# Product pairs in turns by k tile, norm steps two products apart, and bias loads ahead of the first queries

## The chip, the cores and the metric

The kernel runs on one core of a Trainium2 chip. The metric is the device time of one execution in microseconds, from which the median of several runs is taken. All stretches below are microseconds from the start of the profiled span.

## What is computed

Two transformer-like blocks run one after the other on 512 tokens of width 1024, in float32. The first block is a normed input product into three mixers (a gated convolution of width 31 with a norm per head, a short gated convolution, a spatial gating with a norm per head), an output product, a layer of 16384 experts chosen by product keys, and a gated projection. The second block is a state-space mixer with a gated output product, a convolutional feed-forward layer, a gated projection, a differential attention with relative bias, a second feed-forward layer and a second gated projection. Cut to what the change touches:

```python
def group_layernorm(x, g, b, heads):                  # the mixers' norm per head
    m = jnp.mean(xf, axis=-1, keepdims=True)
    var = jnp.mean(jnp.square(xf - m), axis=-1, keepdims=True)
    ...
z = rmsnorm(h, g_mix[i]) @ w_in[i]                    # and so each stage: norm, then products
y = causal_dwconv(val * jax.nn.sigmoid(gate), w)      # 31 taps, then group_layernorm, then silu
mixed = jnp.einsum("hij,bnjhc->bnihc", ws, vb) + b_s  # after group_layernorm of v
bias = rel_bias[t5_causal_bucket(rel)]                # tables used by the attention, much later
```

## The kernel before

Activations lie with features on partitions: eight k tiles of 128 features by 512 tokens. A weight strip holds 128 output features for all eight k tiles. Each float32 product is made of three matmuls of reduced form (L161 high weights by high input, L162 low weights by high input, L163 high weights by low input). The high half of a weight strip is copied by ScalarE (L148, `wh`), the low half is the difference made by VectorE or, for strips marked `pool`, by GpSimd (L150, `wl`). The input's high half is made by ScalarE (L117, L119), its low half by VectorE (L112, L114). So L163 is the matmul that waits when an input tile comes late.

The order on every engine is the order in which the program issues; nothing reorders it. Time in the program is counted in ticks, one after each product of eight k tiles (24 matmuls). `later(n, f)` runs `f` n ticks on, `lin` makes one product, and `done` ticks, puts the product's follow-up one tick on and runs some background work from `self.bg`. `lin2` makes the first two products of a stage and leaves their last k tile to the end, because the tile of the previous stage that is finished last is k tile 7. It is called ten times: mixers (L527, with `first=True`), expert queries, the three gated projections, the state-space input, the gated output product, the two feed-forward layers, the attention queries. Only with `first=True` do the two products go in turns, the second two k tiles behind the first; otherwise the first product's k tiles 0 to 6 go ahead of the second's. Behind the first product's last tile stands the norm's sum over features (L240), behind the second's its spread over partitions (L252); the follow-ups need both.

`head_ln` (L332) is the mixers' norm of one head pair: mean by a matmul (L339, `pmn`), centring on VectorE and squaring on ScalarE one tick on, `two_rms` one tick on (L361 `psv`, a root, a reciprocal and a split on VectorE into `rl`), then the turn (L374, `pst`) one tick on and the spread (L381, `psb`) one tick on. It runs for three tiles of the convolution (issued one tick after the last of 31 taps, L442, `cacc`) and three of the gating (`vv`). Seven taps are issued per product as background work. `two_rms` is also used by the attention's norms, with a lag of one tick.

In the expert stage the background list begins with `bias_prep` (L1740): GpSimd loads `rel_bias`, negates it, then loads the buckets and the lambdas; eight tables (`head`, L1761 on TensorE) and one small step follow; writes of zeros (L655) are set between them, and a copy of an index table comes last.

Of the kernel before, what the change touches and what calls it, by code (L numbers as in the profile page):

```python
# [14 lines left out]
ALU = mybir.AluOpType  # L15
# [21 lines left out]
class K:  # L37
# [142 lines left out]
            c = slice(k * P, k * P + P)  # L180
            self.mm3(ps, s.hi[:, c], s.lo[:, c], *rhs[k], k == 0, k == len(rhs) - 1)

    def lin2(self, rhs, *posts, first=False):

        n = len(rhs)
        ss = [self.next_strip(), self.next_strip(self.LA - 1)]
        pss = [self.mm() for _ in posts]
        if first:
            for k in range(n + 1):
                for i, j in ((0, k), (1, k - 2)):  # L190
                    if 0 <= j < n - 1:
                        self.prod(pss[i], ss[i], rhs, j, j + 1)
        else:
            for s, ps in zip(ss, pss):
                self.prod(ps, s, rhs, 0, n - 1)
        for s, ps, post in zip(ss, pss, posts):
            self.prod(ps, s, rhs, n - 1, n)
            self.done(post, ps)
# [133 lines left out]
    def head_ln(self, y, out):  # L332

        nc = self.nc
        d = {}

        def mean():
            d["m"] = self.px_(name="pmn")
            nc.tensor.matmul(d["m"], self.bd64, y, start=True, stop=True)  # L339
            self.later(1, center)  # L340

        def center():
            nc.vector.tensor_tensor(y, y, d["m"], ALU.subtract)
            d["sq"] = self.tmp(tag="sq")
            nc.scalar.activation(d["sq"], y, AF.Square)
            self.later(1, lambda: self.two_rms(d["sq"], self.sel2, 1.0, scale))

        def scale(psb):
            yn = self.tmp(tag="yn")
            nc.vector.tensor_tensor(yn, y, psb, ALU.mult)  # L350
            out(yn)

        mean()

    def two_rms(self, sq, sel, scale, out):

        nc = self.nc
        d = {}
        ps = self.px_((P, NB, 2), "psv")
        for b in range(NB):  # L360
            nc.tensor.matmul(ps[:, b, :], sq[:, b * P : b * P + P], sel, start=True, stop=True)  # L361
        r = self.sp.tile([P, NB, 2], F32, tag="rl", name=self.name("rl"), bufs=3)
        nc.scalar.activation(r, ps, AF.Sqrt, scale=scale, bias=self.eps)
        r2 = self.sp.tile([P, NB, 2], F32, tag="rl2", name=self.name("rl2"), bufs=3)
        nc.vector.reciprocal(r2, r)

        r4 = self.sp.tile([P, NB, 4], F32R, tag="rl4", name=self.name("rl4"), bufs=3)
        nc.vector.tensor_copy(r4[:, :, 0:2], r2)
        nc.vector.tensor_tensor(r4[:, :, 2:4], r2, r4.bitcast(F32)[:, :, 0:2], ALU.subtract)

        def turn():
            pst = self.px_((4, NB, P), "pst")
            for b in range(NB):
                nc.tensor.transpose(pst[:, b, :], r4.bitcast(F32)[:, b, :], self.ident)  # L374
            d["t"] = self.tmp((4, T), F32R, tag="rT")
            nc.scalar.copy(d["t"], pst.rearrange("p a b -> p (a b)"))
            self.later(1, spread)

        def spread():
            psb = self.px_(name="psb")  # L380
            nc.tensor.matmul(psb, self.selT, d["t"], start=True, stop=True)  # L381
            out(psb)

        self.later(1, turn)

    TAPS = 7
    W_IN_ORDER = [0, 3, 1, 15, 4, 2, 16, 8, 5, 17, 10, 6, 12, 9, 11, 13, 7, 14]
# [11 lines left out]
    def mix_in(self, after):  # L399
        nc, I = self.nc, self.I  # L400
# [10 lines left out]
        xn = self.rhs(self.xn[0])  # L411
# [20 lines left out]
        def conv(j, sg):  # L432
            y = self.loc(tag="ypad", bufs=3)
            nc.vector.tensor_tensor(y, st["val", j], sg, ALU.mult)
            acc = self.loc(tag="cacc", bufs=3)

            def tap(k):
                w, o = cw[:, j * 31 + k : j * 31 + k + 1], 30 - k
                if k == 30:
                    nc.scalar.activation(acc, y, AF.Identity, scale=w, bias=cb[:, j : j + 1])  # L440
                else:
                    nc.vector.scalar_tensor_tensor(out=acc[:, o:], in0=y[:, : T - o], scalar=w, in1=acc[:, o:], op0=ALU.mult, op1=ALU.add)  # L442
                if k == 0:
                    self.later(1, lambda: self.head_ln(acc, lambda yn: ln_a(j, yn)))

            tap(30)
            self.bg += [(1, lambda k=k: tap(k)) for k in range(29, -1, -1)]

        def ln_a(j, yn):
            nc.scalar.activation(yn, yn, AF.Silu, scale=self.v("ln_a_g")[:, j : j + 1], bias=self.v("ln_a_b")[:, j : j + 1])  # L450
            self.split(mix[:, j, 0, :], mix[:, j, 1, :], yn)
# [67 lines left out]
        posts = {}  # L519
# [4 lines left out]
        self.bg_rate, self.credit = self.TAPS, 0  # L524
        self.norm_stat(st)
        o = self.W_IN_ORDER
        self.lin2(xn, posts[o[0]], posts[o[1]], first=True)  # L527
        for m in o[2:]:
            self.lin(xn, posts[m])
        self.run_bg(1000)  # L530
# [93 lines left out]
    def peer(self):  # L624
        nc, I = self.nc, self.I
# [12 lines left out]
        iota = self.loc((P, P), tag="iota")  # L638
        nc.scalar.dma_start(iota, I["c_iota"])

        iotaP = self.bank("mmc", (P, P), "held")
# [3 lines left out]
        sq = self.tc.tile_pool(name="pq", bufs=1)  # L645
        self.st = sq.__enter__()
        sk = self.loc((P, 16, P), tag="sk")
        nc.scalar.dma_start(sk, I["skT"])
        self.bg = self.bias_prep() + [(0.1, lambda: nc.scalar.copy(iotaP, iota))]
        zero = self.loc((P, 112), tag="zero")  # L650
        nc.gpsimd.memset(zero, 0.0)
        zd = self.m1d.rearrange("g c t m -> (g c t) m").rearrange("(p b) m -> p b m", p=P)[:, :, 0:112]
        for i in range(8):
            o = zd[:, 8 * i : 8 * i + 8, :]
            self.bg.insert(2 * i + 1, (0, lambda o=o: nc.gpsimd.dma_start(o, zero.unsqueeze(1).to_broadcast([P, 8, 112]))))  # L655
        n = self.ap.tile([P, KT, 2, TD], F32R, tag="xn", name="n", bufs=2)
# [1084 lines left out]
    def bias_prep(self):  # L1741

        nc, I = self.nc, self.I
        self.bd = self.dp.tile([8, P, 640], F32, name="biasd")
        rb = self.loc((33, 8), tag="rb")
        oh = self.loc((33, 640), tag="rboh")
        lq = self.loc((P, 4, 64), tag="lq")
        self.nlam = self.cp.tile([P, 1], F32, name="nlam")

        def loads():  # L1750
            nc.gpsimd.memset(rb, 1e30)
            nc.gpsimd.dma_start(rb[0:32, :], I["rel_bias"])
            nc.gpsimd.tensor_scalar(out=rb[0:32, :], in0=rb[0:32, :], scalar1=-1.0, scalar2=None, op0=ALU.mult)
            nc.gpsimd.dma_start(oh, I["c_buckets"])
            nc.gpsimd.dma_start(lq, I["lam"])

        def head(h):
            o = self.loc((P, 640), tag="rbo", bufs=2)
            for a, b in ((0, 512), (512, 640)):
                ps = self.px_(name="pb")  # L1760
                nc.tensor.matmul(ps[:, 0 : b - a], rb[:, h : h + 1].to_broadcast([33, P]), oh[:, a:b], start=True, stop=True)  # L1761
                nc.scalar.copy(o[:, a:b], ps[:, 0 : b - a])
            nc.gpsimd.dma_start(self.bd[h], o)

        def lam():
            pr = self.loc((P, 2, 64), tag="lpr")
            nc.vector.tensor_tensor(pr, lq[:, 0:2], lq[:, 2:4], ALU.mult)
            sm = self.loc((P, 2), tag="lsm")
            nc.vector.tensor_reduce(sm, pr, AX.X, ALU.add)
            nc.scalar.activation(sm, sm, AF.Exp)  # L1770
            nc.vector.tensor_tensor(self.nlam, sm[:, 1:2], sm[:, 0:1], ALU.subtract)
            nc.vector.tensor_scalar(out=self.nlam, in0=self.nlam, scalar1=-self.LAM_INIT, scalar2=None, op0=ALU.add)

        return [(0.1, loads)] + [(0.1, lambda h=h: head(h)) for h in range(8)] + [(0.1, lam)]

    def head_rms(self, y, gain, then):

# [403 lines left out]
```

## Time and profile before

| what | value |
|---|---|
| median of 3 runs | 3077.76 us (3073.26 to 3085.12) |
| profiled execution | 3078.27 us, span 3076.5 us |
| mean granted TensorE clock | 0.971 of full speed |
| TensorE busy | 95% of the span |
| VectorE, ScalarE, GpSimd busy | 72%, 42%, 36% |

The page gives shares over the whole span. The stages have different limits, so the change is read stage by stage: from the list of who waits for whom, then from sums over stretches, then from the instructions in order of time. In a timeline a row is start, duration, engine, line, operation, what it writes and reads, how many are merged, and in brackets the idle time ahead of it and what ended it. A matmul's duration overlaps with the next; what one costs is the distance between starts, 0.227 us at the full clock of 2.4 GHz and 0.427 us at 1.2 GHz.

### The profile page before, as it was taken

The page shows a single profiled execution, that of the slowest core. Times are in us where ns is not written, and L with a number is a line of the kernel's source. Part 1 is how long each engine was busy: PE and PEld are TensorE (multiplying, and loading weights), DVE is VectorE, ACT ScalarE, POOL GpSimd, SP SyncE. Part 2 cuts the span into 40 slices and gives each one's busy share as a digit, 9 for nine tenths or more (in the row PEclk, how much of TensorE's full clock was granted, in tenths as well). Part 3 has the DMA queues.
Part 4 walks back from the last instruction along what each step waited for, and adds up shares of the span by engine and source line. Part 5 has one row for each costly group of instructions (what it writes and reads, how often), then busy time and mean ns, then how long its engine had stood idle before and what let it go on. Part 6 is the DMA issues. An engine that isn't in the chain of part 4 may idle for free. (4 is left out here: it accounts for less than half of the span.)

```text
span 3076.5 us, 39413 instructions
## 1 busy us (share of the span) xinstructions
PE 2908.9 (95%) x14359; PEld 2445.6 (79%) x14359; DVE 2218.9 (72%) x3788; ACT 1303.4 (42%) x2209; POOL 1093.8 (36%) x936
## 2 busy tenths in 40 slices
PE   8999988889999999999999979999999998999998
PEld 6677888788887888888787768888877766888886
DVE  7945888986888889988886674666666356566665
ACT  4333246566433433443335343433344345433333
POOL 3224566653248778877872321000011011100001
PEclk9889999899999999999999989999999989999999
DMA  4124335679778988898894473233332211333323
GB/s 140 48 83 148 97 129 186 232 245 313 252 263 313 336 318 322 331 350 315 312 328 147 125 225 103 77 102 99 99 97 95 77 42 42 96 103 96 96 72 99
DMA packets 235067, 534.77 MB, mean 174 GB/s; under 512 B 35135, under 2 KB 127683, under 8 KB 222202
## 3 DMA queue, kind: packets, MB, share of 16 engines
q1 hardware_dynamic: 170570, 343.69, 33.9%
q0 software_dynamic: 24832, 140.74, 12.4%
q10 hardware_dynamic: 39472, 47.84, 4.5%
q8 instruction: 113, 1.85, 0.2%
q14 instruction: 80, 0.66, 0.1%
HBM read 468.75 MB, written 63.44 MB: 173 GB/s over the span
## 5 line engine op out<-in xcount | busy, mean ns | idle before, releaser
L150 DVE TENSOR_TENSOR wl<-wr,wh 128x1024 fp32r<-128x1024 f32 (+2 forms) x453 | 545.3, 1213 | 510.1 <-ACT wh L148 509.9
L148 ACT ACTIVATE wh<-wr 128x1024 fp32r<-128x1024 f32 (+2 forms) x552 | 544.7, 995 | 403.7 <-PE mm L163 196.2
L161 PE MATMUL mm<-xn,wh 128*128 128x512 f32 x1296 | 520.9, 402 | 14.3 <-ACT xn L119 8.9
L163 PE MATMUL mm<-xn,wh 128*128 128x512 f32 x1296 | 512.4, 395 | 5.8 <-DVE xn L114 5.8
L162 PE MATMUL mm<-xn,wl 128*128 128x512 f32 x1296 | 512.1, 395 | 1.9 <-POOL wl L150 1.9
L230 POOL TENSOR_TENSOR accs<-accs,sq 128x512 f32<-128x512 f32 x56 | 86.3, 1541 | 1042.7 <-ACT sq L229 1038.4
L1112 PE MATMUL pv<-wh,A 128*128 128x512 f32 x1536 | 437.5, 397 | 15.8 <-ACT A L117 5.9
L150 POOL TENSOR_TENSOR wl<-wr,wh 128x1024 fp32r<-128x1024 f32 x99 | 241.3, 2439 | 449.1 <-ACT wh L148 446.6
L161 PE MATMUL mm<-n,wh 128*128 128x384 f32 x1024 | 350.6, 342 | 0.8 <-ACT gs L705 0.8
L162 PE MATMUL mm<-n,wl 128*128 128x384 f32 x1024 | 345.6, 337 | 5.9 <-DVE wl L150 4.3
L1112 PEld LDWEIGHTS pv<-wh,A 128*128 128x128 f32 x1536 | 286.8, 189 | 80.6 <-DVE A L112 11.0
L163 PE MATMUL mm<-n,wh 128*128 128x384 f32 x1024 | 345.9, 338 | 3.1 <-DVE n L114 3.1
L161 PEld LDWEIGHTS mm<-xn,wh 128*128 128x128 f32 x1296 | 248.5, 192 | 69.3 <-ACT xn L119 8.9
L163 PEld LDWEIGHTS mm<-xn,wh 128*128 128x128 f32 x1296 | 247.7, 191 | 61.4 <-DVE xn L114 8.3
L162 PEld LDWEIGHTS mm<-xn,wl 128*128 128x128 f32 x1296 | 248.4, 192 | 55.2 <-POOL wl L150 2.3
L1112 PE MATMUL pv<-wl,A 128*128 128x512 f32 x768 | 241.9, 396 | 9.4 <-DVE wl L150 9.3
L117 ACT ACTIVATE A<-ga 128x384 fp32r<-128x384 f32 x128 | 67.3, 526 | 357.7 <-DVE ga L1076 357.7
L162 PEld LDWEIGHTS mm<-n,wl 128*128 128x128 f32 x1024 | 194.2, 190 | 9.7 <-DVE wl L150 5.6
L161 PEld LDWEIGHTS mm<-n,wh 128*128 128x128 f32 x1024 | 194.5, 190 | 4.9 <-issue 1.4
L163 PEld LDWEIGHTS mm<-n,wh 128*128 128x128 f32 x1024 | 194.0, 189 | 3.4 <-DVE n L114 3.4
L1112 PEld LDWEIGHTS pv<-wl,A 128*128 128x128 f32 x768 | 144.0, 189 | 49.0 <-DVE wl L150 17.3
L1670 ACT ACTIVATE uc<-up,vec 128x512 f32<-128x512 f32 x88 | 71.8, 816 | 203.8 <-DVE up L1668 203.8
(414 smaller groups left out, 5438.9 us busy)
## 6 DMA issues: line engine op xcount, KB each, us to landing
wr<-in_exp_u SPq DMA_DIRECT2D x128, 512.0 KB, 5.4
wr<-in_exp_v SPq DMA_DIRECT2D x128, 512.0 KB, 6.9
wr<-in_w_up SPq DMA_DIRECT2D x88, 512.0 KB, 3.6
gd<-gb ACTq DMA_DIRECT2D x48, 512.0 KB, 5.0
G<-gd SPq DMA_DIRECT2D x32, 768.0 KB, 6.3
wr<-in_w_dn SPq DMA_DIRECT2D x64, 320.0 KB, 2.9
wr<-in_w_pg SPq DMA_DIRECT2D x24, 512.0 KB, 4.2
sd<-gs SPq DMA_DIRECT2D x56, 192.0 KB, 2.9
```

The lines of the kernel that those rows point to most:

```text
L117: nc.scalar.activation(hi, src, AF.Copy)
L148: nc.scalar.activation(s.hi, s.raw, AF.Copy)
L150: eng.tensor_tensor(s.lo, s.raw, s.hi.bitcast(F32), ALU.subtract)
L161: t.matmul(ps, wh, xh, start=start, stop=False)
L162: t.matmul(ps, wl, xh, start=False, stop=False)
L163: t.matmul(ps, wh, xl, start=False, stop=stop)
L230: self.later(1, lambda: nc.gpsimd.tensor_tensor(acc, acc, sq, ALU.add))
L1112: nc.tensor.matmul(pv[2 * b + h], a[:, x, o], w[:, h * T : h * T + T], start=(e == 0 and i == 0 and w is s.hi), stop=last)
L1670: nc.scalar.activation(c, u, AF.Identity, scale=w(2), bias=cb[:, m : m + 1])
```

## The change

`lin2` always goes in turns, and the switch `first` is gone. In the mixers' norm the turn is issued two ticks after `two_rms` instead of one, and a convolution's norm two ticks after its last tap instead of one. The three bias loads are issued at the start of the expert stage, ahead of the first query product, with `rel_bias` last; the negation is a background step of its own and on VectorE; the copy of the index table is the first background step.

```diff
-    def lin2(self, rhs, *posts, first=False):
+    def lin2(self, rhs, *posts):
...
-        if first:
-            for k in range(n + 1):
-                for i, j in ((0, k), (1, k - 2)):
-                    if 0 <= j < n - 1:
-                        self.prod(pss[i], ss[i], rhs, j, j + 1)
-        else:
-            for s, ps in zip(ss, pss):
-                self.prod(ps, s, rhs, 0, n - 1)
+        for k in range(n + 1):
+            for i, j in ((0, k), (1, k - 2)):
+                if 0 <= j < n - 1:
+                    self.prod(pss[i], ss[i], rhs, j, j + 1)
...
-            self.later(1, lambda: self.two_rms(d["sq"], self.sel2, 1.0, scale))
+            self.later(1, lambda: self.two_rms(d["sq"], self.sel2, 1.0, scale, 2))
...
-    def two_rms(self, sq, sel, scale, out):
+    def two_rms(self, sq, sel, scale, out, lag=1):
...
-        self.later(1, turn)
+        self.later(lag, turn)
...
-                    self.later(1, lambda: self.head_ln(acc, lambda yn: ln_a(j, yn)))
+                    self.later(2, lambda: self.head_ln(acc, lambda yn: ln_a(j, yn)))
...
-        self.bg = self.bias_prep() + [(0.1, lambda: nc.scalar.copy(iotaP, iota))]
+        bias, loads = self.bias_prep()
+        loads()
+
+        self.bg = [(0.1, lambda: nc.scalar.copy(iotaP, iota))] + bias
...
         def loads():
+            nc.gpsimd.dma_start(oh, I["c_buckets"])
+            nc.gpsimd.dma_start(lq, I["lam"])
             nc.gpsimd.memset(rb, 1e30)
             nc.gpsimd.dma_start(rb[0:32, :], I["rel_bias"])
-            nc.gpsimd.tensor_scalar(out=rb[0:32, :], in0=rb[0:32, :], scalar1=-1.0, scalar2=None, op0=ALU.mult)
-            nc.gpsimd.dma_start(oh, I["c_buckets"])
-            nc.gpsimd.dma_start(lq, I["lam"])
+
+        def negate():
+            nc.vector.tensor_scalar(out=rb[0:32, :], in0=rb[0:32, :], scalar1=-1.0, scalar2=None, op0=ALU.mult)
...
-        return [(0.1, loads)] + [(0.1, lambda h=h: head(h)) for h in range(8)] + [(0.1, lam)]
+        return [(0.1, negate)] + [(0.1, lambda h=h: head(h)) for h in range(8)] + [(0.1, lam)], loads
```

## Rows read from the trace of the kernel before

**Rows 1.** The page: busy time, share of the span and instructions of each engine.
```profile
PE 2908.9 (95%) x14359; PEld 2445.6 (79%) x14359; DVE 2218.9 (72%) x3788; ACT 1303.4 (42%) x2209; POOL 1093.8 (36%) x936
```
**Rows 2.** TensorE's waits over the span: total, times, longest, in microseconds.
```profile
PE pmn L339 <- DVE cacc L442: 6.2, 1, 6.2
...
PE mm L163 <- DVE xn L114: 5.8, 5, 2.4
```
**Rows 3.** Sums over stretches, pair to L240: length, busy (instructions), clock, DMA, GB/s.
```profile
225.04:235.24 10.20, 10.20 (x47) 8.45 (x45) 3.50 (x3) 3.48 (x4) 7.86 (x8) 1.00 0.61 201
1667.26:1678.23 10.97, 10.52 (x47) 8.37 (x45) 9.04 (x8) 6.57 (x10) 7.65 (x5) 1.00 0.09 19
1720.71:1737.40 16.69, 13.68 (x46) 10.43 (x45) 11.24 (x11) 9.88 (x15) 11.69 (x9) 0.80 0.02 10
...
2343.22:2356.33 13.11, 10.79 (x47) 8.34 (x45) 10.03 (x12) 7.01 (x10) 4.33 (x3) 1.00 0.17 52
```
**Rows 4.** Timeline, state-space pair: TensorE's wait, VectorE's low halves, GpSimd's last sum.
```profile
1728.71 0.79 PE L163 MATMUL mm<-xn,wh 128*128 128x512 f32 x1 [2.41 <-DVE xn L114]
...
1726.90 3.44 DVE L114 SCALAR_TENSOR_TENSOR xn<-x,gfs,xn 128x512 fp32r<-128x512 f32 x2
...
1731.44 2.25 POOL L1982 TENSOR_TENSOR accs<-accs,sq 128x512 f32<-128x512 f32 x1
```
**Rows 5.** Timeline, attention's pair: TensorE's wait, its norm steps, VectorE's low halves.
```profile
2350.52 0.50 PE L163 MATMUL mm<-xn,wh 128*128 128x512 f32 x1 [2.03 <-DVE xn L114]
...
2358.76 0.48 PE L161 MATMUL mm<-xn,wh 128*128 128x512 f32 x1
...
2348.72 3.45 DVE L114 SCALAR_TENSOR_TENSOR xn<-x,vec,xn 128x512 fp32r<-128x512 f32 x2
```
**Rows 6.** Timeline of VectorE: the second strip's low half in the second gated projection.
```profile
2289.78 1.72 DVE L150 TENSOR_TENSOR wl<-wr,wh 128x1024 fp32r<-128x1024 f32 x1
```
**Rows 7.** Timeline of the expert stage's start: GpSimd's bias loads, TensorE.
```profile
232.71 0.73 POOL L1752 DMA_DIRECT2D rb<-in_rel_bias  x1 [0.31 <-POOL rb L1751]
236.78 0.24 POOL L1753 TENSOR_SCALAR rb<-rb 32x8 f32<-32x8 f32 x1 [3.34 <-DMA rb<-in_rel_bias]
...
235.24 0.95 PE L240 MATMUL px<-ones,accs 128*128 128x1 f32 x8
239.52 2.13 PE L1761 MATMUL pb<-rboh,rb 33*128 33x512 f32 x4 [3.34 <-DMA rboh<-in_c_buckets]
...
254.18 1.05 PE L679 MATMUL sc<-sk,q 128*128 128x128 f32 x8
...
255.16 2.42 PE L1761 MATMUL pb<-rboh,rb 33*128 33x512 f32 x8
```
**Rows 8.** Sums over two stretches behind that wait, columns as in rows 3.
```profile
236.20:250.12 13.92, 10.60 (x26) 7.15 (x27) 1.47 (x3) 5.24 (x11) 5.70 (x8) 0.63 0.43 129
250.12:260.00 9.88, 9.88 (x46) 7.50 (x45) 4.42 (x24) 3.24 (x8) 6.82 (x7) 1.00 0.58 199
```
**Rows 9.** Sums over stretches of the mixers, columns as in rows 3 (TensorE, weights, VectorE, ...).
```profile
37.60:154.40 116.80, 106.18 (x464) 79.18 (x462) 112.83 (x138) 37.64 (x50) 33.61 (x14) 0.91 0.19 61
...
72.63:79.46 6.83, 5.16 (x11) 2.64 (x12) 6.62 (x11) 1.53 (x2) 2.51 (x1) 0.50 0.15 59
...
113.40:185.40 72.00, 72.00 (x291) 48.91 (x291) 51.40 (x72) 25.31 (x34) 7.61 (x3) 0.79 0.16 52
```
**Rows 10.** Timeline, mixers: TensorE's first wait; VectorE around it; a split by GpSimd.
```profile
74.30 1.01 PE L374 MATMUL pst<-ident,rl 128*4 128x128 f32 x4 [3.76 <-DVE rl L369]
...
74.06 0.68 DVE L417 TENSOR_TENSOR vv<-mm,rstd 128x512 f32<-128x512 f32 x1
74.67 7.25 DVE L442 SCALAR_TENSOR_TENSOR cacc<-ypad,vec,cacc 128x483 f32<-128x483 f32 x7
...
82.43 5.41 DVE L442 SCALAR_TENSOR_TENSOR cacc<-ypad,vec,cacc 128x506 f32<-128x506 f32 x7
...
76.95 2.84 POOL L150 TENSOR_TENSOR wl<-wr,wh 128x1024 fp32r<-128x1024 f32 x1 [6.13 <-ACT wh L148]
```

More of the change, by code (lines that the diff above doesn't have):

```diff
@@ L526, in mix_in @@
         o = self.W_IN_ORDER
-        self.lin2(xn, posts[o[0]], posts[o[1]], first=True)
+        self.lin2(xn, posts[o[0]], posts[o[1]])
         for m in o[2:]:
```

## Prediction

> **What bounds the kernel now.** I read the shares of the page first: TensorE is busy for 95% of the span [rows 1], so its holes are all that a change of order can give back. Then the list of TensorE's waits, in which the change aims at three kinds: the low half of an input tile that comes late at a stage's start (5.8 us, five times), the convolution's last tap (6.2 us, once) [rows 2], and the start of the expert stage, where TensorE waits 3.34 us for a DMA [rows 7]. Then sums over stretches, to see what each wait costs behind it: after the DMA wait the granted clock is 0.63 in the mean over 13.92 us, though nothing is idle there but the 3.34 us, and 1.00 in the stretch after it [rows 8]. So a wait costs its own time and half of the time for which the clock then stands at 1.2 instead of 2.4 GHz. Last the timeline of each place. The mixers differ from the rest: from 37.60 to 154.40 VectorE is busy for 112.83 of 116.80 us [rows 9], so there VectorE is the limit and TensorE's waits are its shadow.
>
> **The pairs in turns.** Nine pairs change; the mixers' pair already goes so. The work, the strips and their DMAs are the same and are issued at the same point, so no queue but TensorE's changes. Unhindered, the 45 matmuls up to L240 take 10.20 us [rows 3], 0.227 us each. In turns, k tile 6 of the first product comes eleventh instead of seventh, and its L163 starts 32 matmuls in, after 7.25 us, instead of 20 in, after 4.5 us; 13 matmuls (2.95 us) follow it to L240.
> The second strip is needed 2.0 us in instead of 4.8. The nearest case is the second gated projection: its low half ends at 2291.50 [rows 6], the pair starts 2290.60, so it is needed at 2292.6. No new wait.
> In six of the nine pairs nothing is late (the first line of rows 3 stands for them): nought.
> First gated projection: 10.97 against 10.20 us [rows 3]; 0.7 us gained, 0 to 0.8.
> Attention: tile 6 would be asked for at 2343.22 + 7.25 = 2350.47 and is there at 2350.52; L240 comes at 2353.5 instead of 2356.33 [rows 3, 5], and tile 7 is there by 2352.17 [rows 5]. 2.9 us gained; 2.3 if only the two idle pieces go.
> State-space input: asked for at 1720.71 + 7.25 = 1727.96, there at 1728.71 [rows 3, 4]: 0.75 us of wait stay, and L240 comes at 1731.7 instead of 1737.40. But what is late next is GpSimd's second sum of squares, which ends at 1733.69 [rows 4] and is read behind L240. L240 takes about 0.9 us, so the second sum's matmul starts at 1733.7 instead of about 1738.3: 4.5 us gained. Part of that is the clock: 0.80 in the mean over this pair [rows 3], 0.20 of 16.69, which is 3.3 us. If two waits of 0.75 and 1.2 us still let it fall, only 1.2 us are left; if the sum were not needed so early, 5.7.
> Sum of the pairs: 8.1 us. Behind each stand stages in which everything hangs on this chain, so the gain is passed on to the end.
>
> **The bias loads.** Before, GpSimd issues `rel_bias` at 232.71, waits 3.34 us for it, negates, and only then issues the buckets, which the first table's matmul awaits: TensorE stands from 236.18 to 239.52 [rows 7]. After, all three loads are issued when GpSimd is through with the norm's sums. It is busy for 7.86 of the 10.20 us of the pair and then splits a strip, so I put the loads at about 230, three issues of 0.73 us at most to 232.2, and the last landing 3.34 us later, 235.5. L240 is at 235.24, its root and reciprocal take to 236.7, and the negation comes behind these on VectorE, so it finds its data. Behind the negation on VectorE are queued the multiplications by the norm for q, which need L252 anyway; behind the loads on GpSimd are queued the zero fill and the third query strip's split, 2.2 us later than before but with TensorE's need for it still some 3 us away. Each table moves one product back, because the copy of the index table takes the first place in the background list.
> Now the sum from L240 to the first scores (L679): before, 235.24 to 254.18, 18.94 us [rows 7]. After: L240 to the following product's first matmul 2.43 us, as in the attention (2356.33 to 2358.76) [rows 3, 5]; one table, half of 2.42 us for two [rows 7], 1.21; 24 matmuls, 5.46. That is 9.10, a gain of 9.84, of which one table comes back later, 1.21: 8.6 us. Ends: 3.3 (the idle alone goes and the clock falls all the same) and 9.8. I take 8.6, as the same kind of small matmuls with two tables runs at clock 1.00 in the next stretch [rows 8].
>
> **The mixers.** Nothing is removed; steps move one product back. The first wait is 3.76 us for the reciprocal's split [rows 10]. When that turn moves, the next in TensorE's queue is the mean of the second `vv`, which VectorE finishes at 74.74 [rows 10]: the wait is not gone but 0.4 us longer. The second wait, 6.20 us for the last tap, comes one product (5.46 us) later and nearly vanishes; but VectorE's end at 154.40 stays, and the squares and centred tiles that TensorE asks for next hang on the same VectorE queue. What counts is how much earlier TensorE starts the 72.00 us that it then works without a hole, 113.40 to 185.40 [rows 9]. The bound on the gain is one product, 5.5 us.
> Against that stand three costs. The last convolution head now has its mean behind the last input product and its turn in the drain, between the first and the last k tiles of the output product, where no product hides the transposes (1.01 us) and the copy behind them, which I put at the same: 1 to 2 us more. ScalarE's queue no longer waits for the first turn, so the weight copy behind it, and with it GpSimd's split, comes ahead of that `vv`. Seven taps take 7.25 us with a split among them and 5.41 without [rows 10]: the split costs VectorE 1.8 us, and TensorE's wait grows by that. And new waits let the clock fall: 0.50 for 6.83 us behind the first one, 3.4 us lost [rows 9].
> The Trainium skill speaks against this part: SBUF — State Buffer, section "SBUF: two separate sides", says that VectorE and GpSimd share a port pair as an exclusive lock, and that whichever comes second is blocked for the whole instruction. By that rule a split moved ahead would hold a waited-for step for the split's full length, 2.84 us here, not 1.8; the sum would be 1 us worse. The trace shows the lock, at the smaller price.
> Half a product gained (2.7), 1.5 lost in the drain, 1.8 lost to the split: 0.6 us of loss, which I take as nought. Ends: 5.5 gained, 6 lost.
>
> **The sum.** 8.1 + 8.6 + 0 = 16.7 us off the profiled execution's 3078.27, which lies 0.5 us above the median: 3061.6 in its terms, 3061 against the median of 3077.76.
>
> **The rivals.**
> (a) The mixers gain as meant: both waits go (3.8 and 6.2) with 3.4 us of low clock each, less 3 in the drain, 13.8 in all: 3047. For it: TensorE is full from 113.40 on. Against: VectorE at 97% before that.
> (b) The clock falls at the expert stage's start without a wait, as the L240, L252 and table matmuls are small: only 3.3 us there, 3066. For it: the stretch with clock 0.63 holds just these. Against: rows 5 and 8.
> (c) The lock between VectorE and GpSimd decides in the mixers: two splits come ahead of waited-for steps (3.6 us) with one more fall of the clock (3.4) and the drain: 8 us lost, 3069. This is the result that the rule above would bring, in this trace's prices.
> (d) Slower: in the mixers each of the four norm tiles that had no wait gets one like that of rows 10, as the lags set TensorE's steps behind VectorE steps that come one product later as well: 4 x (3.8 + 3.4) = 29 us, total 12 us over before, 3090. It decides from a loss of 16.7 us in the mixers on, the third such wait.
>
> **How the numbers follow.** Forecast 0.55 (3055 to 3067), (a) 0.10, (b) 0.13, (c) 0.17, (d) 0.05. Leaving out (d), the outer half of (a) and the tail of (c): 3051 to 3073. A measurement of this kernel tells 0.5% (15.4 us) from no change, which is 3062.4. Faster by more: six tenths of the forecast, (a), and a little of (b), 0.45. Slower by more, above 3093: 0.03. Within: 0.52.
>
> **What would show it.** Right: the three late pairs take 10.2 to 11.8 us up to L240 with waits under 1 us at L163, and a wait for GpSimd appears ahead of L1993; the first tables run behind L252 without a wait and the clock there is 1.00; in the mixers a wait of 4 to 6 us stands ahead of `pmn` of `vv` near 74, and the output product starts within 3 us of 177.9. Wrong: a table waiting for `rel_bias`, low clock from 236 on, or mixers that end more than 6 us away from before.

## The result, and the profile after

The changed kernel takes 3061.49 us in the median (3058.84 to 3066.78), the kernel before 3077.76 (3070.24 to 3090.27). The medians differ by 16.3 us. The ratio, taken from all runs, is 0.9942, with a 95% interval of 0.9925 to 0.9958: 17.9 us faster, 12.9 to 23.1. The profiled execution has a span of 3059.7 us, against 3076.5 before.

First TensorE's waits of the changed kernel (engine, line and operand, what released it: total, times, longest). They answer to [rows 2].

```profile
PE pmn L335 <- DVE vv L413: 6.9, 2, 6.2
...
PE pmn L335 <- DVE cacc L438: 1.1, 1, 1.1
PE px L1994 <- POOL accs L1983: 1.0, 1, 1.0
...
PE mm L163 <- DVE xn L114: 0.6, 1, 0.6
```

The wait for the low half of an input tile was 5.8 us in five pieces and is 0.6 in one. The wait for the convolution's last tap was 6.2 us and is 1.1. Two of the waits shown are new: 6.2 us for a `vv`, and 1.0 us for GpSimd's second sum of squares; a third of 1.9 us, for squares in the mixers, stands further below.

Then the sums over the three pairs that had been late, from the pair's first matmul to the first matmul of the norm's sum (L236 here, L240 before), and over the expert stage's start up to the first scores. Columns as in [rows 3]: length, busy time and instructions of TensorE, weight loads, VectorE, ScalarE and GpSimd, then the mean granted clock, the DMA share and GB/s.

```profile
1660.57:1670.80 10.23, 10.23 (x47) 8.45 (x45) 9.05 (x8) 6.57 (x10) 7.66 (x5) 1.00 0.02 7
1713.27:1724.38 11.11, 10.49 (x46) 8.38 (x45) 10.52 (x11) 9.55 (x15) 9.72 (x7) 1.00 0.04 15
2330.10:2340.54 10.44, 10.44 (x46) 8.38 (x45) 10.08 (x12) 7.02 (x10) 4.39 (x3) 1.00 0.05 18
234.19:243.71 9.52, 9.52 (x49) 7.53 (x48) 1.53 (x4) 5.41 (x11) 5.67 (x5) 1.00 0.63 201
```

They were 10.97, 16.69 and 13.11 us [rows 3] and 18.94 [rows 7]. The clock is 1.00 in all four, and TensorE is idle only in the second. The timeline shows where, and how the bias loads now lie (start, duration, engine, line; in brackets the idle time before and its releaser):

```profile
1721.30 0.50 PE L163 MATMUL mm<-xn,wh 128*128 128x512 f32 x1 [0.62 <-DVE xn L114]
...
1724.38 0.95 PE L236 MATMUL px<-ones,accs 128*128 128x1 f32 x8
1726.35 1.05 PE L1994 MATMUL px<-ones,accs 128*128 128x1 f32 x8 [1.02 <-POOL accs L1983]
...
228.78 0.75 POOL L1750 DMA_DIRECT2D rboh<-in_c_buckets  x1
...
230.56 0.53 POOL L1753 DMA_DIRECT2D rb<-in_rel_bias  x1 [0.29 <-POOL rb L1752]
...
235.57 0.15 DVE L1756 TENSOR_SCALAR rb<-rb 32x8 f32<-32x8 f32 x1
...
236.86 1.34 PE L1762 MATMUL pb<-rboh,rb 33*128 33x512 f32 x4
```

In the state-space pair 0.62 us of the wait for the input tile are left, and 1.02 us for GpSimd's sum come behind it. In the expert stage the negation is through at 235.72, and the first table follows at 236.86 with no idle time before it.

Last the mixers. The first three waits of TensorE, and ahead of the first of them the VectorE steps and a split by GpSimd:

```profile
74.83 2.08 PE L335 MATMUL pmn<-vv,bd 128*128 128x512 f32 x2 [6.22 <-DVE vv L413]
...
114.06 1.10 PE L335 MATMUL pmn<-cacc,bd 128*128 128x512 f32 x2 [1.13 <-DVE cacc L438]
...
117.47 1.05 PE L357 MATMUL psv<-sel,sq 128*128 128x2 f32 x8 [1.88 <-ACT sq L341]
...
66.68 6.97 DVE L438 SCALAR_TENSOR_TENSOR cacc<-ypad,vec,cacc 128x487 f32<-128x487 f32 x4
73.57 0.20 DVE L361 RECIPROCAL rl<-rl 128x8 f32<-128x8 f32 x1
...
74.09 0.68 DVE L413 TENSOR_TENSOR vv<-mm,rstd 128x512 f32<-128x512 f32 x1
...
69.83 2.54 POOL L150 TENSOR_TENSOR wl<-wr,wh 128x1024 fp32r<-128x1024 f32 x1 [0.94 <-ACT wh L148]
```

VectorE finishes that `vv` at 74.77 us, as it did before (74.74 [rows 10]). TensorE no longer waits for the reciprocal; it waits for the next thing that VectorE makes. The four taps from 66.68 on take 6.97 us, with GpSimd's splits beside them. The split at 69.83 is one that lay behind this `vv` before (76.95 [rows 10]). What its new place costs can be read against the kernel with the pairs alone (first experiment below), which has the old lags:

```profile
72.09 1.01 PE L370 MATMUL pst<-ident,rl 128*4 128x128 f32 x4 [3.75 <-DVE rl L365]
...
71.86 0.68 DVE L413 TENSOR_TENSOR vv<-mm,rstd 128x512 f32<-128x512 f32 x1
```

There TensorE stops at 68.34 us, 44.66 behind the norm's sum ahead of the mixers, and the `vv` is finished 4.20 us later (72.54). In the changed kernel TensorE stops at 68.61, 44.67 behind that sum, and the `vv` is finished 6.16 us later. So the split that moved ahead costs VectorE 2.0 us. The traces of all kernels with splits on GpSimd agree: 4.2 us in the five that have the turn's old lag, 6.2 in the six that have the new one.

### The profile page after: what moved, and what is told of

Same layout as the page of the kernel before. It is cut to its first block, busy times and chain, and to the rows that moved or that the text cites. A ratio compares the mean times of both kernels' runs of the same rounds, so it can differ in the third digit from the quotient of the medians.

```text
span 3059.7 us, 39415 instructions
## 1 busy us (share of the span) xinstructions
PE 2905.5 (95%) x14359; PEld 2445.8 (80%) x14359; DVE 2221.5 (73%) x3789; ACT 1303.6 (43%) x2209; POOL 1092.2 (36%) x935
```

## The experiments

Each kernel was timed against the kernel before on the same chip. "Mixers" below is the time from the norm's sum ahead of the mixers to the one behind them (24.34 to 235.24 us in the kernel before: 210.90). "Expert part" is the time from there to the norm's sum of the first gated projection (1442.99 us in the kernel before).

**The pairs alone.** In `lin2`:

```diff
-        if first:
+        for k in range(n + 1):
...
-        else:
-            for s, ps in zip(ss, pss):
-                self.prod(ps, s, rhs, 0, n - 1)
```

> The kernel before with the pairs in turns and nothing else. My theory (the terms add up, each in its own stage): 8 us faster, ratio 0.9974; to be read in the trace, first gated projection 0.7 us and first state-space pair 4.5 us and attention pair 2.7 us earlier at their L240, the start of the expert stage unchanged at 18.9 us from L240 to the first scores. Rival: the terms need one another, because a stage that starts earlier finds its strips or its clock in another state; then the state-space pair gives 5.7 or 1.2 instead of 4.5, and the total is 5 us or less. Second rival: what changes between the two state-space and expert stages is scatter of the expert stage, which in the changed kernel gave back some 6 us between 400 and 1660 us; then this kernel moves there too, by some us of either sign, though nothing in that stretch has been changed.

Ratio 0.9988 (0.9976 to 0.9999): 3.7 us faster, 0.3 to 7.4, so the 8 us that I expected lie outside. In its trace the three pairs take 10.23, 11.12 and 10.43 us up to the norm's sum, as in the changed kernel. The second rival, that the expert stage moves of itself, does not show: the lead over before is 2.25 us at 372 us and 2.14 at 1660. Up to the norm's sum the pairs do what the sum says. But 24 matmuls behind it the state-space pair has won 2.9 us on the kernel before and not 4.5, as the clock falls there (0.86 in the mean over 12.20 us). More of the reason shows when the same pairs are read in kernels that have them in the old order. The sums over the state-space pair and the attention pair of the kernel with the bias loads alone, and the last wait in each on the timeline:

```profile
1708.08:1723.49 15.41, 12.38 (x47) 9.52 (x46) 11.27 (x11) 9.88 (x15) 11.73 (x9) 0.89 0.04 14
2330.72:2346.73 16.01, 13.69 (x47) 10.42 (x46) 10.02 (x12) 7.00 (x10) 4.32 (x3) 0.79 0.14 43
```

```profile
1716.10 0.77 PE L163 MATMUL mm<-xn,wh 128*128 128x512 f32 x1 [2.41 <-DVE xn L114]
...
2338.02 0.79 PE L163 MATMUL mm<-xn,wh 128*128 128x512 f32 x1 [2.03 <-DVE xn L114]
```

The sum over the state-space pair of the kernel with the lags alone, and the wait in it:

```profile
1721.47:1735.31 13.84, 10.81 (x46) 8.34 (x45) 11.29 (x11) 9.89 (x15) 11.75 (x9) 1.00 0.04 13
```

```profile
1729.49 0.50 PE L163 MATMUL mm<-xn,wh 128*128 128x512 f32 x1 [2.41 <-DVE xn L114]
```

The waits are those of the kernel before to a hundredth (0.6 and 2.4 us; 2.03 us). But the state-space pair takes 16.69, 15.41 or 13.84 us, with a mean clock of 0.80, 0.89 or 1.00, and the attention pair 13.11 or 16.01, with 1.00 or 0.79. The same wait is followed by a fall of the clock in one execution and not in the next. Where the clock stays up in both orders, the turn order shortens the state-space pair by 2.7 us (13.84 to 11.12) and the attention pair by as much (13.1 to 10.44); behind the state-space pair the wait for GpSimd's sum takes 1.2 of them back.

That wait can be followed by a fall as well, and this shows in one and the same kernel: the sums from the norm's sum over the next 24 matmuls in the changed kernel, first in the execution above, then in a second one (last but one in this section).

```profile
1724.38:1735.08 10.70, 9.51 (x58) 8.08 (x57) 6.11 (x10) 4.50 (x8) 2.01 (x3) 1.00 0.24 73
1726.65:1738.92 12.27, 11.11 (x58) 9.64 (x56) 6.09 (x10) 4.45 (x8) 1.96 (x3) 0.86 0.21 66
```

The waits in both are 0.62 us for the input tile and 1.0 for GpSimd's sum. Of the seven kernels with the turn order and this sum on GpSimd, the clock falls here in four (0.86 each) and stays at 1.00 in three. So the turn order trades a longer wait with a fall that comes now and then for a shorter one with a fall that comes now and then.

**The bias loads alone.** In `bias_prep` and at the head of the expert stage:

```diff
-            nc.gpsimd.tensor_scalar(out=rb[0:32, :], in0=rb[0:32, :], scalar1=-1.0, ...
+        def negate():
+            nc.vector.tensor_scalar(out=rb[0:32, :], in0=rb[0:32, :], scalar1=-1.0, ...
...
-        self.bg = self.bias_prep() + [(0.1, lambda: nc.scalar.copy(iotaP, iota))]
+        bias, loads = self.bias_prep()
+        loads()
+        self.bg = [(0.1, lambda: nc.scalar.copy(iotaP, iota))] + bias
```

> The kernel before with the bias loads at the start of the expert stage (and the negation on VectorE, the index copy first), and nothing else. My theory: from L240 to the first scores 9.5 us instead of 18.9, no wait of a table for a DMA, granted clock 1.00 there; 8.6 us faster at about 290 us from the start. If the gain is passed on, the whole is 8.6 us faster, ratio 0.9972. Rival: the later half of the expert stage is bound by something that does not start earlier (strips that come by DMA, their copies and splits), and gives 4 to 6 us of it back between 900 and 1660 us, as the changed kernel did; then the whole is 3 to 5 us faster, ratio 0.9985 to 0.9990.

Ratio 0.9962 (0.9948 to 0.9976): 11.7 us faster, 7.4 to 16.0; the 8.6 that I expected lie inside. From the norm's sum to the first scores 9.51 us at a clock of 1.00. The lead over before is 9.4 us larger at the first scores than ahead of the stage, 8.0 at 294 us, and 10.8 at 372 us. The end of the expert part shows no return of 4 to 6 us: the part takes 1431.87 us, 11.1 less than before. The rival falls.

**The lags alone.** In `head_ln` and `conv`:

```diff
-            self.later(1, lambda: self.two_rms(d["sq"], self.sel2, 1.0, scale))
+            self.later(1, lambda: self.two_rms(d["sq"], self.sel2, 1.0, scale, 2))
...
-                    self.later(1, lambda: self.head_ln(acc, lambda yn: ln_a(j, yn)))
+                    self.later(2, lambda: self.head_ln(acc, lambda yn: ln_a(j, yn)))
```

> The kernel before with both lags in the mixers, and nothing else. My theory (VectorE is the limit there, so waits only move): the wait for the reciprocal near 70.5 us becomes one of about 4.2 us for the second vv, the wait for the last tap at 107 us shrinks to 1 or 2 us, and at the residual add behind the mixers the kernel stands within 1.5 us of before; total within 2 us of before, ratio 1.000. Rival: the lags remove the waits as meant, 10 to 14 us faster by the end of the mixers, ratio 0.996. Second rival: the exclusive use of the port by VectorE and GpSimd makes it 6 to 8 us slower, ratio 1.002.

Ratio 0.9997 (0.9985 to 1.0009): between 4.6 us faster and 2.8 slower. The waits lie where the changed kernel has them (6.24 us for the second `vv`, 1.15 for the last tap, 1.87 for the squares), and the mixers take 211.22 us against 210.90. Both waits that the lags aim at are gone, and nothing is won: my theory holds, both rivals fall.

**The change without the lags.** The two lines above the other way round, in the changed kernel.

> The changed kernel with the lags of the mixers as before (pairs in turns and bias loads only). My theory: the lags cost about 0.9 us (in the changed kernel 1.92 us of lead at 70 us had become 1.05 at 194), so this one is 0.9 us faster than the changed kernel, 17.5 us faster than before, ratio 0.9943, which a comparison of totals can't tell from the changed kernel; the trace must show the lead of 1.9 us kept until 235 us. Rival: the gain of the two parts is less than their sum, 10 to 13 us, and the lags bring the rest by shifting where later stages fall; then the ratio is 0.996 or above. On the expert stage: if its loss of 6 us between 400 and 1660 us is scatter, this kernel shows another figure there, although it differs from the changed kernel only before 190 us; if it is bound by a stream, the same 6 us.

Ratio 0.9952 (0.9936 to 0.9968): 14.8 us faster, which agrees with the changed kernel's 17.9 within the intervals, and with the sum of the two parts, 15.4. It does not exclude the rival's 0.996 or a little above. The trace did not show the lead of 1.9 us kept: the mixers took 211.88 us, though they are the mixers of the kernel before. Four kernels with these mixers took 209.0 to 211.9 us (mean 210.3); five with both lags 209.1 to 213.0 (mean 211.3). The 0.9 us that I had read off two traces is inside that scatter.

**One lag at a time**, in the kernel before. First the turn:

```diff
-            self.later(1, lambda: self.two_rms(d["sq"], self.sel2, 1.0, scale))
+            self.later(1, lambda: self.two_rms(d["sq"], self.sel2, 1.0, scale, 2))
```

> The kernel before with the lag of the norm's turn alone (two products), the convolution's head as before. To be read between the first L240 and the L240 behind the mixers, 210.90 us before and 209.0 to 211.9 us in three other kernels with the same mixers. My theory (VectorE is the limit, TensorE only waits in another place): the wait of 3.76 us before the first turn becomes one of 6.2 us before the second vv's mean, the wait of 6.2 us for the last tap stays, and the turn of the last head comes later: 212 to 220 us, slower by 2 to 9. Rival (each lag removes the wait it aims at): the 3.76 us and the low clock behind it go, 205 to 208 us.

Then the convolution's head:

```diff
-                    self.later(1, lambda: self.head_ln(acc, lambda yn: ln_a(j, yn)))
+                    self.later(2, lambda: self.head_ln(acc, lambda yn: ln_a(j, yn)))
```

> The kernel before with the lag of the convolution's head alone, the turn as before. Same stretch as for the turn's lag. My theory (VectorE is the limit): the wait of 6.2 us for the last tap shrinks to under 2 us, but VectorE passes its last tap at the same time, so that other waits take the place; 209 to 215 us. Rival (each lag removes its wait): 6.2 us and the low clock behind it go, 202 to 206 us.

The turn alone: ratio 1.0044 (1.0030 to 1.0058), mixers 223.4 us, 13 slower. The head alone: 1.0022 (1.0006 to 1.0038), mixers 221.7, 11 slower (the whole kernel by 6.8, between 1.8 and 11.7). Both are further on the slow side than I expected (up to 220 and 215). TensorE's longer waits in the mixers, first with the turn's lag, then with the head's lag, and behind these two VectorE steps of the second kernel:

```profile
74.58 2.08 PE L339 MATMUL pmn<-vv,bd 128*128 128x512 f32 x2 [6.22 <-DVE vv L417]
113.86 2.05 PE L339 MATMUL pmn<-cacc,bd 128*128 128x512 f32 x2 [5.94 <-DVE cacc L442]
127.16 0.69 PE L481 MATMUL pmx<-wsT,vT 128*64 128x128 f32 x2 [3.05 <-DVE yn L350]
```

```profile
74.66 0.60 PE L374 MATMUL pst<-ident,rl 128*4 128x128 f32 x4 [3.74 <-DVE rl L369]
...
130.54 0.69 PE L481 MATMUL pmx<-wsT,vT 128*64 128x128 f32 x2 [8.79 <-DVE yn L350]
...
124.48 5.41 DVE L442 SCALAR_TENSOR_TENSOR cacc<-ypad,vec,cacc 128x508 f32<-128x508 f32 x7
129.81 0.68 DVE L350 TENSOR_TENSOR yn<-cacc,psb 128x512 f32<-128x512 f32 x1
```

The new wait in both stands at L481, the spatial product, which must wait until VectorE has read an earlier tile of the ring that `pmx` is taken from. That read, L350, is queued behind seven taps (124.48 to 129.81). Neither the kernel before nor the changed one has such a wait. I read it so, by the program: with the lags unequal, the steps of `vv` and of `cacc` meet in another order in the ring, and a tile is held over seven taps. That the order is the cause was not tried by itself.

**The mixers' strips split by VectorE**, in the changed kernel:

```diff
         self.order += [Strip(self.I["w_in"][m], KT) for m in self.W_IN_ORDER]
-        for s in self.order[2:]:
-            s.pool = True
```

> The changed kernel with the strips of the mixers split by VectorE instead of GpSimd; all else the same. It measures the disputed price of a split that runs beside VectorE. In the changed kernel 12 such splits lie between 37.6 and 154.4 us, and the VectorE step beside each takes about 2.0 us longer (a tap 2.7 us instead of 0.73). On VectorE itself a split takes 1.2 us. My theory (VectorE is the limit there, and GpSimd blocks it for 2.0 us a split): 12 x 0.8, 8 to 10 us faster by the end of the mixers, 201 to 203 us between the two L240 instead of 210.25, ratio to before 0.991. Rival (the splits on GpSimd are nearly free, VectorE only shows the wait; or VectorE, in order, now stands and waits for ScalarE's copies): VectorE has 12 x 1.2 = 14 us more to do, 4 to 14 us slower, ratio 0.9955 to 0.999.

Ratio 0.9919 (0.9893 to 0.9946), mixers 200.51 us, 9.74 less than in the changed kernel and just below the 201 to 203 that I expected. VectorE's taps and splits between 24 and 190 us, by line (shapes and count, then busy us, mean ns of one, and the idle time before them), first in the changed kernel, then in this one:

```profile
L438 DVE SCALAR_TENSOR_TENSOR cacc<-ypad,vec,cacc 128x511 f32<-128x511 f32 (+14 forms) x90 | 89.7, 998 | 3.8 <-ACT cacc L436 1.1
L150 DVE TENSOR_TENSOR wl<-wr,wh 128x1024 fp32r<-128x1024 f32 x4 | 4.9, 1221 | 0.7 <-ACT wh L148 0.7
```

```profile
L436 DVE SCALAR_TENSOR_TENSOR cacc<-ypad,vec,cacc 128x511 f32<-128x511 f32 (+14 forms) x90 | 65.9, 734 | 2.9 <-ACT cacc L434 0.3
L150 DVE TENSOR_TENSOR wl<-wr,wh 128x1024 fp32r<-128x1024 f32 x21 | 25.5, 1220 | 8.1 <-ACT wh L148 8.1
```

The durations of a tap (count, then ns: least, median, most), in the same order:

```profile
L438 DVE SCALAR_TENSOR_TENSOR cacc<-ypad,vec,cacc x90: 711/737/2928, 35.7 to 153.7; 128x511 f32<-128x511 f32 x3, 128x510 f32<-128x510 f32 x3, 128x509 f32<-128x509 f32 x3, 128x508 f32<-128x508 f32 x3
```

```profile
L436 DVE SCALAR_TENSOR_TENSOR cacc<-ypad,vec,cacc x90: 711/734/751, 33.5 to 139.9; 128x511 f32<-128x511 f32 x3, 128x510 f32<-128x510 f32 x3, 128x509 f32<-128x509 f32 x3, 128x508 f32<-128x508 f32 x3
```

And the sums over the mixers, in the same order:

```profile
23.94:234.19 210.25, 199.02 (x838) 149.75 (x839) 153.19 (x187) 73.42 (x97) 59.62 (x32) 0.89 0.23 74
```

```profile
21.46:221.97 200.51, 195.58 (x840) 148.07 (x839) 144.09 (x201) 73.66 (x97) 21.81 (x17) 0.91 0.25 77
```

Without splits on GpSimd no tap takes more than 0.75 us; with them some take up to 2.93. The 90 taps lose 23.8 us in all, nearly all of it in twelve taps that take 2.0 us longer each, while the 17 more splits on VectorE cost it 20.6 (two of them only because this kernel is further on at 190 us). Over the mixers VectorE is busy for 9.1 us less with more work. Its last tap ends 119.2 us behind the norm's sum instead of 130.5, and the mixers are 9.7 us shorter: what VectorE gains TensorE gains, nearly, which is what "VectorE is the limit" means. TensorE waits for no low half of a strip in the mixers of either kernel, so the gain is not that strips come sooner. In the totals the intervals of the two kernels overlap; the gain rests on the mixers, 199.8 to 200.5 us in three kernels with these splits on VectorE against 209.0 to 213.0 in nine with them on GpSimd and the lags changed in both or in neither. The norm's sum ahead of them comes 2.5 us earlier too (21.46 against 23.94).

**The same without the lags** (the two lines of the lags as before, strips split by VectorE).

> The kernel with the mixers' strips split by VectorE, and both lags back to one product. With the lags the mixers take 200.51 us between the two L240. Theory A (the lags bought nothing only because VectorE, held up by GpSimd's splits, was the limit): with VectorE freed a wait for a reciprocal and one for a last tap are real again, each with some low clock behind it, 204 to 212 us. Theory B (the lags are worth nothing in any case, as VectorE stays the limit): 199 to 202 us.

Ratio 0.9911 (0.9886 to 0.9936), mixers 200.22 us: theory B. One wait of the old kind is back:

```profile
98.78 1.10 PE L335 MATMUL pmn<-cacc,bd 128*128 128x512 f32 x2 [3.37 <-DVE cacc L436]
```

and with the lags there is one of 2.4 us for a `vv` at 89.85 instead. The lags are worth nothing in either kernel. That VectorE is still the reason in this one was not tried by itself.

**The last sum on VectorE**, in the changed kernel:

```diff
-            self.later(1, lambda: nc.gpsimd.tensor_tensor(acc2, acc2, sq, ALU.add))
+            eng = nc.vector if k == KT - 1 else nc.gpsimd
+            self.later(1, lambda: eng.tensor_tensor(acc2, acc2, sq, ALU.add))
```

> The changed kernel with the last addition of the second sum of squares (k tile 7, state-space input) on VectorE instead of GpSimd. My theory (that sum is what is late next in the state-space pair): the wait of 1.02 us before the second sum's matmul goes, and the following products come 1.0 us earlier against L240, from 1724.38 us and the first product behind it at 1731: 1.0 us, ratio unchanged within the measurement. Rival: the state-space pair's own wait of 0.62 us grows, because the addition stands ahead of the low half in VectorE's queue; then nothing is gained.

Ratio 0.9937 (0.9913 to 0.9961). The wait for the input tile is still 0.62 us, and the second sum follows the first without one:

```profile
1723.86 1.03 PE L1995 MATMUL px<-ones,accs 128*128 128x1 f32 x8
```

The next product starts 1.71 us behind the norm's sum instead of 2.88, so 1.2 us are won there. In this execution a fall of the clock took them back (0.85 in the mean; 24 matmuls later it is 0.5 us behind the changed kernel); in the last kernel below it did not. As a total it can't be told from nothing.

**The index copy last**, in the changed kernel:

```diff
-        self.bg = [(0.1, lambda: nc.scalar.copy(iotaP, iota))] + bias
+        self.bg = bias + [(0.1, lambda: nc.scalar.copy(iotaP, iota))]
```

> The changed kernel with the copy of the index table last in the background list, as before, so that the first table is asked for one product earlier. If only the idle time and the clock were at stake: 18.94 - 3.34 - 5.1 = 10.5 us from L240 to the first scores instead of 9.5, and the table that no longer comes later gives the 1.2 us back by 290 us: no difference there. Rival: the first table meets the negation too early and waits for it on VectorE by 0.3 to 1 us, and the clock falls for it, 1 to 5 us slower.

Ratio 0.9970 (0.9956 to 0.9984), the rival. The timeline of the first table and of the negation that it waits for, and then the sum from the norm's sum to near the first scores:

```profile
234.67 1.31 PE L1762 MATMUL pb<-rboh,rb 33*128 33x512 f32 x4 [0.67 <-PE px L236]
...
234.43 0.14 DVE L1756 TENSOR_SCALAR rb<-rb 32x8 f32<-32x8 f32 x1
```

```profile
233.05:243.50 10.45, 9.78 (x41) 7.34 (x40) 1.53 (x4) 5.15 (x11) 3.58 (x5) 0.84 0.64 201
```

The negation stands behind the norm's reciprocal on VectorE and ends at 234.57, 0.1 us before the table. The row puts the wait down to the norm's sum, which was through at 234.0; of what the table needs, the negation is what ends last. The wait is 0.67 us, and the clock falls to 0.84 in the mean; from the norm's sum to the first scores it is 13.08 us instead of 9.52, and the lead gained between 232 and 372 us is 7.5 us instead of 10.8. These 3.3 us are traced. The ratios differ by more (0.0028, 8.6 us), and I can't place the rest: on the chip of this run the changed kernel itself, in the one execution that follows, took 3067.71 us against 3068.24 here, so the totals alone do not show a loss.

**The changed kernel once more.**

> The changed kernel once more, for the scatter from execution to execution. My theory (a wait of the same length is followed by a fall of the clock in some executions and not in others, and the expert stage's length scatters for the same reason): the mixers take 209 to 212 us, the lead of 11.8 us over before at 372 us changes by another figure than 5.1 up to 1660 us, between 0 and 6. Rival (the expert stage gives 5 us back for a reason that lies in the change): 5.1 within half a us.

3067.71 us in one execution. Mixers 213.02 us, above the 209 to 212 that I expected; expert part 1435.22 against 1436.61. Of its lead at 372 us it gave back 2.2 us up to 1660, not 5.1; the change without the lags gave back 1.4. So that loss is no part of the change.

**The last two together**: strips split by VectorE and the last sum on VectorE.

> The changed kernel with two more edits: the mixers' strips split by VectorE, and the last addition of the second sum of squares on VectorE. If they add up: 9.7 us in the mixers and 1.0 in the state-space pair, 10.7 us faster than the changed kernel, ratio to before 0.989. If the state-space stage takes the 1.0 us back with a fall of the clock, 0.992.

3046.74 us (3042.66 to 3052.22), ratio 0.9902 (0.9881 to 0.9923): 30 us faster than before, with an interval that lies below the changed kernel's and holds both 0.989 and 0.992. Mixers 199.75 us; the second sum again without a wait, and here the clock stays up behind it.

## Why the prediction was right, step by step

**The total.** 3061 was forecast, 3061.49 measured; the three parts alone sum to 3.7 + 11.7 + 0.9 = 16.3 us, against 16.7 forecast. That the figures agree this closely is luck: the nine executions of the changed kernel lie between 3058.84 and 3066.78 us, and errors of the terms cancel, as the pairs were put too high (8.1 us; 3.7 by themselves, 0.3 to 7.4) and the bias loads rather low (8.6 us; 11.7 by themselves, 7.4 to 16.0). The terms, part by part, between the first two traces and as means over the traces of all kernels with the old and with the new part (in the state-space row without the two that have the last sum on VectorE, in the expert row without the index copy last):

| part | forecast | between the two first traces | over all kernels |
|---|---|---|---|
| first gated projection | 0.7 | 0.74 | 0.74 |
| state-space pair, to 24 matmuls behind it | 4.5 | 4.41 | 2.5 (old 23.1 to 26.3, new 21.6 to 23.2) |
| attention pair | 2.9 | 2.67 | 3.5 (old 13.1 to 16.0, new 10.4) |
| expert part, less the gated projection | 8.6 | 5.6 | 10.2 (old 1442 to 1444, new 1427 to 1437) |
| mixers | 0 | 0.65 gained | 1.0 lost (old 209.0 to 211.9, new 209.1 to 213.0) |

Between the two first traces these parts make 14.1 of the 16.8 us by which the spans differ; the other 2.7 lie in stretches for which nothing was forecast (0.4 ahead of the mixers, 1.3 behind the state-space pair, 1.0 behind the attention pair).

**The pairs.** The order of what comes late was right: 0.62 us of the low half's wait (0.75 forecast), then GpSimd's sum with 1.02 (1.2 forecast), and nothing in the attention. The state-space term was mis-sized in one respect: 3.3 of its 4.5 us were the clock, which I took as the wait's fixed price. It is a price paid in some executions only, and in the new order as well: the case that the prediction named, two short waits that still let the clock fall, came in four of seven traces. With the clock up in both orders the term is 1.5 us (23.1 against 21.6), near the 1.2 that the prediction left without the clock. Over five kernels with the old order and seven with the new one the term is 2.5 us; the attention, where I counted no clock, gave 3.5 because it fell there in two of five. Together 6.8 against 8.1, inside the 0.3 to 7.4 us that the pairs alone were worth.

**The bias loads.** 9.52 us from the norm's sum to the first scores (9.10 forecast): 2.67 for the norm's steps instead of 2.43, 1.27 for the table (1.21), 5.58 for the products (5.46). The table that comes back later costs 1.5 us (1.2). No clock fell there in any kernel in which the first table came without a wait, and it did fall for 0.67 us of wait with the index copy last; rival (b) falls. What I did not foresee: TensorE's wait for the next norm at 319 us shrinks from 3.1 to 1.9. The copy of the index table, which I had only as a cost of 1.2 us, is what keeps the table behind the negation and so carries 3 us of the gain.

**The mixers.** Nought was forecast, as the sum of half a product gained, a longer drain and a split moved ahead, and with VectorE as the limit. The steps were seen: the first wait turns into one for `vv`, VectorE reaches the last tap at 154.46 us as before at 154.41, the last head's turn waits 0.66 us in the drain, and TensorE, 1.9 us ahead of before at 70 us, is 1.7 ahead at the output product and 1.1 at 190. The 1.9 us at 70 us are not the lags' work: 0.4 was there at the norm's sum, and kernels with the old lags come to this place as early behind that sum (44.66 us). The wait for `vv` was 6.2 us and not 4.2, because one split of GpSimd moved ahead of it, as the prediction had it: that costs VectorE 2.0 us (1.8 forecast). Rivals (a) and (d) fall: nothing was won, and one wait of 1.9 us was added, not four of 3.8. Rival (c) falls too: its 8 us of loss did not come, though its price was real for the split ahead of `vv`. Twelve of 15 splits on GpSimd in that stretch lengthen a tap, by 2.0 us each, near the 1.8 that I used. By the Trainium skill, SBUF — State Buffer, section "SBUF: two separate sides", whichever of the two engines comes second waits for the other's whole instruction, where VectorE reads two inputs from SBUF, as a tap does. The longest tap, 2.93 us against 0.74, agrees with that; the price in the mean, 2.0 us, is below a split's 2.5.

## What to carry to other kernels

Where an engine is busy for 97% of a stretch, moving the steps of the engine that waits for it may only change the name of the wait, as it did here; take work, or a neighbour that lengthens its steps, off the busy engine instead. Try a lag that feeds two interleaved chains in both at once as well as in each: here each half cost 11 to 13 us in its stretch, and the whole nothing. Price a short wait as its own length for certain and the clock behind it as a chance, and read a term in several executions before trusting its tenths.

## What the runs showed of the hardware

The clock's fall behind a short wait is not fixed. One and the same wait of 2.4 us, in the same instructions, was followed by a mean clock over its pair of 0.80, 0.89 and 1.00 in three kernels that differ only elsewhere; one of 2.03 us by 1.00 and 0.79. In the changed kernel, executed twice, one of 1.0 us was followed by 1.00 and 0.86. With the same instructions throughout, the mixers took 210.25 and 213.02 us, and the expert part 1436.61 and 1435.22. Which event decides it the traces don't tell.

In these mixers a VectorE that does the splits itself is faster than one that has them done by GpSimd beside it: 1.22 us for a split on VectorE, against 2.0 us that a split on GpSimd takes from VectorE when it meets a tap (1.6 in the mean over all 15), and 2.5 us of GpSimd besides.
